# Decoder layer: the recurrence's chain in program order on TensorE, with the second half's preparation placed between its links

## The chip, the cores and the metric

The kernel runs on one core of a Trainium2 chip. The core has a matrix engine (TensorE, in the profile PE, with its weight loads as PEld), a vector engine (VectorE, DVE), a scalar engine (ScalarE, ACT), a general engine (GpSimd, POOL) and SyncE (SP), which here only issues DMAs. Each engine works through its own queue in the order in which the program was built, and semaphores hold an instruction back until what it needs is done. The metric is the device time of one execution in microseconds.

## What is computed

One decoder layer over 1024 tokens of width 1024, in float32. Half of the mixing width is attention in latent form (4 heads), the other half is a recurrence with a state of 64 by 64 for each of 8 heads. Cut to what matters here:

```python
u = rmsnorm(h, norm_pre_g)
p = u @ w_in
p_mla, p_rw, z = split(p)
# attention: latents, rotary parts, causal softmax -> y_mla
ps = p_rw + (token_shift(p_rw) - p_rw) * rw_mu
r, k, v, xw, xa = split(ps)
w_log = -softplus(-(rw_w0 + tanh(xw) @ rw_w2)) - 0.5
a = sigmoid(rw_a0 + xa @ rw_a2)

def step(S, inp):
    r_t, w_t, k_t, v_t, kk_t, a_t = inp
    sa = einsum('bhvk,bhk->bhv', S, -kk_t)
    S = (S * w_t[:, :, None, :] + sa[..., None] * (kk_t * a_t)[:, :, None, :]
         + v_t[..., None] * k_t[:, :, None, :])
    return S, einsum('bhvk,bhk->bhv', S, r_t)

_, ys = lax.scan(step, S0, xs)
y_rw = group_norm(ys) + bonus
out = concat([y_mla, y_rw]) * silu(z) @ w_out
h = h + rmsnorm(out, norm_post_g)
```

## The kernel before

The tokens are worked in two halves of 512. In each half the recurrence is cut into eight chunks of 64 tokens. Inside a chunk everything that doesn't depend on the state is done by matrix products ahead of time, which leaves a chain of eight short iterations that carry the state from chunk to chunk.

The program is a list of named steps, `PROGRAM` (line 129). A letter names a function, the digits are its arguments, the first of them the half:

- `A` (`stage_a`, line 154) loads four blocks of 128 tokens, sums their squares on ScalarE, takes the inverse root on GpSimd (`rstd`, lines 57 and 58, a power), scales on VectorE (line 170), transposes on TensorE (line 177, four transpositions to a tile, eight tiles in a half), and splits the result into a high part `uH` (ScalarE, line 181) and a low part `uL` (VectorE, line 182).
- `X` (`op_x`, `lora_in`, line 235) is the projection that feeds the two low-rank products; for half 0 it also loads their weights (`lora_load`, with splits on GpSimd, lines 232 and 233). A projection (`proj`, line 203) is 24 matmuls of 512 columns on line 210, with weights split on ScalarE (line 190) and GpSimd (line 200).
- `P` and `E` prepare one of four column blocks of a half: three projections and the low-rank products (lines 250 and 251, `lora_mm`), then the chunk products (`units`, lines 346 to 400).
- `I` inverts the chunk triangles (lines 401 to 456; VectorE at 418 to 421, TensorE at 447 and 454, copies at 455 and 456), with data sent through memory to other partitions.
- `C` is the chain (line 458). `N` and `G` are the group norm (line 501, reductions on VectorE, a power on GpSimd at line 510) and the outputs (line 518, transpositions on line 525).
- `Z` and `Y` are gate blocks (`zgate`, `zgate2`), `M` and `T` the attention's inputs and their transpositions (`mla_in`, `mla_tail`, with ScalarE's store copies on line 565), `B`, `U`, `K`, `J`, `Q` and `S` the rotary tables (lines 644 to 680), the attention and the output.

The written order is not the order that runs. The whole layer is built under a scheduler that simulates a timeline (line 41) and puts each engine's instructions in an order of its own; the place in the program is the priority. So work that is written later may be placed ahead of a waiting step, and two groups of one loop may be placed in turns.

One iteration of the chain, for two groups of heads (g of 0 and 1), each with a tile `pc` of its own in PSUM: TensorE multiplies the state, held in `SV`, with `LS` (line 474); ScalarE copies the result to `Rs` (line 476); TensorE does the other half of `LS` (line 480) into the same tile, then `AB` times `Rs` (line 484); ScalarE and VectorE copy that to `SV` (lines 486 and 487); TensorE does `BK` (line 490), VectorE adds it to the decayed state, which GpSimd made (lines 494 and 478), and TensorE ends with line 496, whose result ScalarE copies out (line 499). A link is one of these five groups; each is four matmuls in the program and eight records in the trace. What stands between the links is up to the scheduler.

Of the kernel before, what the change touches and what calls it, by code (L numbers as in the profile page):

```python
# [1 line left out]

# [14 lines left out]
T = 1024  # L17
# [27 lines left out]
def layer(tc, x, pos, w_in, w_out, w_uq, w_ukv, vecs, w2, a2, consts, post_g, out):  # L45
# [9 lines left out]
    def rstd(ss, scale):  # L55

        G.tensor_scalar(ss, ss, scale, EPS, ALU.mult, ALU.add)
        G.tensor_tensor(ss, ss, mhalf[:, 0:ss.shape[-1]], ALU.pow)
# [68 lines left out]
PROGRAM = (
    "A0 X0 Z00 B P00 E00 Z01 P01 E01 Z02 P02 E02 P03 E03 I0 C0 N00 G00 N01 G01 M0 Z03 Z04 Z05 Y06 T0 A1 X1",  # L130
    "P10 E10 Z10 P11 E11 Z11 P12 E12 P13 E13 I1 C1 N10 G10 N11 G11 M1 Z12 T1 Z13 Z14 Z15 Z16 Z17 U K J Q0",
    "Q1 Q2 Q3 S",
)

# [1 line left out]
def recurrence(tc, E):  # L136
# [11 lines left out]
    def col(c):  # L148
        return vec[:, c:c + 1]

    uH = alloc(P1, (128, 8, HALF), "uH", F32R)
    uL = alloc(P1, (128, 8, HALF), "uL", F32R)

    def stage_a(h):

        XT = (("v", "sq"), ("sg", "cs"), ("a", "k"), ("kf", "r"))
        for pr in range(2):
            xs = []
            for q in range(2):
# [5 lines left out]
                    junk = alloc(P1, (128, 512), "q", BF16)  # L165
                    S.activation(junk, xh[i], AF.Square, accum_out=ss[:, i:i + 1])
                G.tensor_tensor(ss[:, 0:1], ss[:, 0:1], ss[:, 1:2], ALU.add)
                E["rstd"](ss[:, 0:1], 1.0 / D)
                for i in range(2):
                    V.tensor_scalar(xh[i], xh[i], ss[:, 0:1], 1.0, ALU.mult, ALU.mult)  # L170
                xs.append(xh)
            for k2 in range(4):
                ps = pj((128, 2, 256))
                for kk in range(2):
                    kb = k2 * 2 + kk
                    for q in range(2):
                        PE.transpose(ps[:, kk, q * 128:(q + 1) * 128], xs[q][kb // 4][:, (kb % 4) * 128:(kb % 4 + 1) * 128], ident)
                for kk in range(2):
                    kb = k2 * 2 + kk
                    sl = slice(pr * 256, pr * 256 + 256)  # L180
                    S.activation(uH[:, kb, sl], ps[:, kk], AF.Copy, scale=col(V_PRE + kb))
                    V.scalar_tensor_tensor(uL[:, kb, sl], ps[:, kk], col(V_PRE + kb),  # L182
                                           uH[:, kb, sl].bitcast(F32), ALU.mult, ALU.subtract)

    def load_w(src, shape):
        wf = alloc(P1, shape, "wf", bufs=3)
# [13 lines left out]
                G.tensor_tensor(wl[:, sl], wf[:, sl], wh[:, sl].bitcast(F32), ALU.subtract)  # L200
        return wh, wl

    def proj(c0):

        wh, wl = load_w(w_in[:, c0:c0 + 128].rearrange("(k p) n -> p k n", p=128), (128, 8, 128))
        ps = pj()
# [1 line left out]
        for kb in range(8):  # L208
            for w_, u_ in ((wh, uH), (wh, uL), (wl, uH)):
                PE.matmul(ps, w_[:, kb], u_[:, kb], start=(n == 0), stop=(n == 23))  # L210
                n += 1
        return ps

    def shifted(ps, vi, tag, bufs):

# [17 lines left out]
            G.tensor_tensor(wl, wf, wh.bitcast(F32), ALU.subtract)  # L233

    def lora_in(h):
        px = shifted(proj(CO_X), V_MU_X, "v", 1)
# [5 lines left out]
        V.tensor_tensor(xw[64:128], th[0:64], xw[0:64].bitcast(F32), ALU.subtract)  # L242
        V.tensor_copy(xa[64:128], px[64:128])
        V.tensor_tensor(xa[0:64], px[64:128], xa[64:128].bitcast(F32), ALU.subtract)
        return xw, xa

    def lora_mm(nm, xx, cb):
        wh, wl = lora[nm]
# [206 lines left out]
                V.tensor_copy(AB[0:32, l, :, 32:64], pG[0:32])  # L455
                S.copy(AB[64:96, l, :, 32:64], pG[64:96])

    def chain(h, gt):

        for g in range(2):  # L460
            for e in range(2):
                G.tensor_copy(gt["g"][g]["SV"][ev[e], 0, e], Sst[ev[e], 2 * g:2 * g + 2])
        for c in range(NCH):

            pcs = [chp((128, 4, 2, 64)) for _ in range(2)]
            Rs = [alloc(P1, (128, 2, 64), "Rs", bufs=2) for _ in range(2)]
            SD = [alloc(P1, (128, 2, 64), "SD", bufs=2) for _ in range(2)]
            parts = []
            for g in range(2):
                LS, BK, AB, SV = (gt["g"][g][k] for k in ("LS", "BK", "AB", "SV"))  # L470
                parts.append((LS, BK, AB, SV, Sst[:, 2 * g:2 * g + 2], gt["Dg"][:, 2 * g:2 * g + 2], pcs[g], Rs[g], SD[g]))
            for LS, BK, AB, SV, St, Dg, pc, R_, D_ in parts:
                for l, e in le:
                    PE.matmul(pc[ev[e], 0, l], LS[:, l, c, e, 0:64], SV[:, c, e, l], start=(l == 0), stop=False,  # L474
                              skip_group_check=True)
                S.copy(R_, pc[:, 0])
                for e in range(2):
                    G.tensor_tensor(D_[ev[e]], SV[ev[e], c, e], bc(Dg[ev[e], :, c:c + 1], (64, 2, 64)), ALU.mult)  # L478
                for l, e in le:
                    PE.matmul(pc[ev[e], 1, l], LS[:, l, c, e, 64:128], SV[:, c, e, l], start=False, stop=False,  # L480
                              skip_group_check=True)
            for LS, BK, AB, SV, St, Dg, pc, R_, D_ in parts:
                for l, e in le:
                    PE.matmul(pc[ev[e], 2, l], AB[ev[e], l, c, 0:64], R_[ev[e], l], start=False, stop=False,
                              skip_group_check=True)
                S.copy(SV[ev[0], c, 0], pc[ev[0], 2])
                V.tensor_copy(SV[ev[1], c, 1], pc[ev[1], 2])  # L487
            for LS, BK, AB, SV, St, Dg, pc, R_, D_ in parts:
                for l, e in le:
                    PE.matmul(pc[ev[e], 3, l], BK[:, l, c, e], SV[:, c, e, l], start=False, stop=False,  # L490
                              skip_group_check=True)
                for e in range(2):
                    dst = SV[ev[e], c + 1, e] if c + 1 < NCH else St[ev[e]]
                    V.tensor_tensor(dst, pc[ev[e], 3], D_[ev[e]], ALU.add)  # L494
                for l, e in le:
                    PE.matmul(pc[ev[e], 1, l], AB[ev[e], l, c, 64:128], SV[ev[e], c, e, l], start=False,
                              stop=True, skip_group_check=True)

                S.copy(SV[:, c, 0], pc[:, 1])
# [561 lines left out]
```

## Time and profile before

| what | us |
|---|---|
| runs of the kernel | 783.88, 789.08, 786.29 |
| their median | 786.29 |
| the profiled execution's own time | 783.81 |
| its span | 782.0 |
| its mean granted TensorE clock (1 is full) | 0.951 |

A row of the profile's order of time gives the start in microseconds, the duration, the engine, the line, the operation, the tile written and the tiles read with their shapes, the count of merged instructions, and in square brackets the time for which the engine sat idle before it, with what ended that. Matmuls overlap in such rows, so the distance from one start to the next tells what a group costs, not its duration. A row of windows gives the stretch, its length, for each of TensorE, weight loads, VectorE, ScalarE and GpSimd the busy time (with the count), and behind them the granted clock, the DMA share and the rate. The stretch from the chain of half 0 to the end of its group norm runs here from about 232 to 354 us.

### The profile page before, as it was taken

What the parts mean: (1) busy time and instruction counts of PE and PEld (TensorE: products, weight loads), DVE (VectorE), ACT (ScalarE), POOL (GpSimd) and SP (SyncE); (2) the same over time, 40 slices, a digit from 0 to 9 for tenths busy, and PEclk for the clock granted to TensorE, in tenths of its full rate; (3) what the DMA queues carried; (4) which work ended last, traced back from release to release, by engine and by line L of the source; (5) the groups of instructions that cost most, each with busy time, mean ns of one, the idle gap of its engine ahead of it and who ended that gap; (6) DMA issues with size and microseconds to landing.
All of it is one profiled execution on the core that took longest, in us unless ns stands there. A gap on an engine that the chain in (4) does not pass through costs nothing. (4 is left out here: it accounts for less than half of the span.)

```text
span 782.0 us, 13855 instructions
## 1 busy us (share of the span) xinstructions
PE 713.0 (91%) x5136; PEld 586.1 (75%) x5136; DVE 466.4 (60%) x943; ACT 347.9 (44%) x877; POOL 331.9 (42%) x478
## 2 busy tenths in 40 slices
PE   2789999999978998889999989799899998899996
PEld 1667877789866776667888967577678997788885
DVE  4756757758925522495866691476497767644333
ACT  6465355343725453344353162426354566632221
POOL 6265645445942554263554374032332237442220
PEclk9999999999998899977999989879999999999999
DMA  6224241254383133043223366411023025144321
GB/s 208 80 69 115 54 114 51 68 151 134 114 187 89 28 108 83 2 89 85 57 68 97 86 171 156 131 44 42 2 55 101 21 89 162 52 166 141 121 82 54
DMA packets 118819, 72.84 MB, mean 93 GB/s; under 512 B 47072, under 2 KB 108256, under 8 KB 118752
## 3 DMA queue, kind: packets, MB, share of 16 engines
q1 hardware_dynamic: 118752, 71.96, 32.5%
q8 instruction: 40, 0.66, 0.4%
q14 instruction: 27, 0.22, 0.1%
HBM read 54.38 MB, written 17.56 MB: 92 GB/s over the span
## 5 line engine op out<-in xcount | busy, mean ns | idle before, releaser
L210 PE MATMUL pj<-uH,w 128*128 128x512 f32 x640 | 215.7, 411 | 3.3 <-DVE uL L182 2.5
L200 POOL TENSOR_TENSOR w<-wf,w 128x256 fp32r<-128x256 f32 x168 | 141.3, 871 | 116.6 <-ACT w L190 106.5
L210 PEld LDWEIGHTS pj<-uH,w 128*128 128x128 f32 x640 | 123.7, 195 | 33.1 <-DVE uL L182 2.9
L210 PE MATMUL pj<-uL,w 128*128 128x512 f32 x320 | 130.2, 407 | 0.0
L210 PEld LDWEIGHTS pj<-uL,w 128*128 128x128 f32 x320 | 62.6, 196 | 14.0 <-issue 0.8
L190 ACT CAST w<-wf 128x1024 fp32r<-128x1024 f32 (+1 forms) x50 | 51.4, 1027 | 28.8 <-PE pj L540 21.3
L478 POOL TENSOR_TENSOR SD<-SV,Dg 64x128 f32<-64x128 f32 x64 | 27.9, 436 | 74.0 <-DVE SV L494 59.9
L854 POOL TENSOR_SCALAR wf<-wf,sm 128x128 f32<-128x128 f32 (+7 forms) x32 | 24.0, 750 | 67.1 <-DVE sm L853 51.9
L198 POOL TENSOR_TENSOR w<-wf,w 128x224 fp32r<-128x224 f32 x32 | 23.8, 775 | 38.8 <-ACT w L190 32.2
L359 PEld LDWEIGHTS wk<-LS,pl 64*128 64x128 f32 x256 | 30.2, 191 | 12.5 <-issue 10.2
L979 DVE TENSOR_TENSOR LS<-pj,LS 128x512 f32<-128x512 f32 x16 | 11.1, 691 | 45.5 <-ACT cq L978 44.3
L359 PE MATMUL wk<-LS,pl 64*128 64x128 f32 x256 | 35.6, 289 | 1.3 <-DVE LS L317 1.2
L850 ACT ACTIVATE wf<-pj,mx 128x512 f32<-128x512 f32 (+3 forms) x48 | 27.7, 583 | 13.5 <-DVE mx L847 9.9
L865 ACT CAST BK<-wk 128x512 fp32r<-128x512 f32 (+3 forms) x48 | 22.4, 485 | 25.2 <-PE wk L863 23.2
L373 PEld LDWEIGHTS wk<-r,pl 64*128 64x128 f32 x256 | 29.5, 196 | 4.4 <-issue 2.9
L373 PE MATMUL wk<-r,pl 64*128 64x64 f32 x256 | 31.2, 284 | 1.2 <-DVE LS L364 1.0
L874 PE MATMUL ch<-BK,LS 128*128 128x256 f32 (+1 forms) x160 | 31.6, 282 | 0.7 <-ACT BK L865 0.7
L487 DVE COPY SV<-ch 64x128 f32<-64x128 f32 x32 | 9.2, 294 | 36.5 <-issue 25.7
L418 DVE TENSOR_TENSOR tmp<-XA 128x31 f32<-128x31 f32 (+15 forms) x62 | 28.2, 454 | 4.4 <-DMA XA<-sa 2.6
L866 DVE TENSOR_TENSOR AB<-wk,BK 128x512 fp32r<-128x512 f32 (+3 forms) x48 | 26.0, 551 | 7.3 <-ACT BK L865 6.8
L420 DVE TENSOR_TENSOR XA<-XA,tmp 128x31 f32<-128x31 f32 (+15 forms) x62 | 28.4, 458 | 1.9
L845 DVE TENSOR_REDUCE mx<-pj 128x1 f32<-128x512 f32 (+3 forms) x48 | 25.8, 551 | 6.0 <-PE pj L844 3.4
(339 smaller groups left out, 1659.4 us busy)
## 6 DMA issues: line engine op xcount, KB each, us to landing
wf<-in_w_in_dram SPq DMA_DIRECT2D x42, 512.0 KB, 3.9
zs<-st SPq DMA_DIRECT2D x16, 256.0 KB, 3.1
wf<-in_x_dram SPq DMA_DIRECT2D x8, 512.0 KB, 3.7
out_dram<-LS SPq DMA_DIRECT2D x16, 256.0 KB, 2.1
wf<-in_w_in_dram SPq DMA_DIRECT2D x8, 448.0 KB, 3.5
bvd<-st SPq DMA_DIRECT2D x8, 256.0 KB, 2.0
SV<-bvd SPq DMA_DIRECT2D x16, 128.0 KB, 3.4
yrw<-SV SPq DMA_DIRECT2D x8, 256.0 KB, 2.6
```

Of the source, the lines that this page charges most:

```text
L190: S.copy(wh, wf)
L200: G.tensor_tensor(wl[:, sl], wf[:, sl], wh[:, sl].bitcast(F32), ALU.subtract)
L210: PE.matmul(ps, w_[:, kb], u_[:, kb], start=(n == 0), stop=(n == 23))
L359: PE.matmul(pE[e][:, ci], pl[r, c4 + ci, 1 - e:3 - e].rearrange("p a b -> p (a b)"), LS[r, c4 + ci, e, :], start=True, stop=True)
L373: PE.matmul(pB[:, c], pl[r, c, 1 - e:3 - e].rearrange("p a b -> p (a b)"), dD[r, c], start=True, stop=True)
L418: V.tensor_tensor(t3, bc(At[:, j, j + 1:32].unsqueeze(2), (128, n, w)), bc(X[:, j, 0:w].unsqueeze(1), (128, n, w)), ALU.mult)
L420: V.tensor_tensor(X[:, j + 1:32, 0:w], X[:, j + 1:32, 0:w], t3, ALU.add)
L478: G.tensor_tensor(D_[ev[e]], SV[ev[e], c, e], bc(Dg[ev[e], :, c:c + 1], (64, 2, 64)), ALU.mult)
L845: V.tensor_reduce(mx[:, n5:n5 + 1], s_, axis=AX.X, op=ALU.min)
L850: S.activation(pr[:, b0:b1], sc[:, 0:b1 - b0], AF.Exp, bias=mx[:, 0:1], scale=-1.0, accum_out=sm[:, n5:n5 + 1])
L866: V.tensor_tensor(PL[:, b0:b0 + nb, o], pt[:, 0:nb], PH[:, b0:b0 + nb, o].bitcast(F32), ALU.subtract)
L874: PE.matmul(py[:, o], l_, r_, start=(j == 0 and n == 0), stop=(j == nk - 1 and n == 2), skip_group_check=True)
```

## The change

Four edits.

1. `stage_a` and `lora_in` become generators: they stop after each four transpositions, and after each two matmuls of a projection. `stage_a` leaves its last instruction on VectorE and on GpSimd in `last`.
2. The chain is wrapped so that TensorE's instructions in it keep the written order among themselves, and it takes an iterator `fill`. It draws one piece from it after line 484's links, one after the last link, and one more after each odd iteration. For half 0 the pieces are `A1` and then `X1`: eight pieces of transpositions and twelve of two matmuls, which is as many as there are places. For half 1 there are none.
3. In the main loop, whatever is written after `A0` is queued behind A0's last instructions on VectorE and on GpSimd, and whatever is written after `C0` is queued behind the chain's last matmul on TensorE.
4. `PROGRAM` is changed: `M0`, the gates and `T0` come before `C0`; `A1` and `X1` are gone as steps of their own; `P10` stands behind the group norms; `Y06` becomes `Z06 Z07`.

```diff
     def rstd(ss, scale):
         G.tensor_scalar(ss, ss, scale, EPS, ALU.mult, ALU.add)
-        G.tensor_tensor(ss, ss, mhalf[:, 0:ss.shape[-1]], ALU.pow)
+        return G.tensor_tensor(ss, ss, mhalf[:, 0:ss.shape[-1]], ALU.pow)
...
-        for op in " ".join(PROGRAM).split():
-            name = op.rstrip("0123456789")
-            ops[name](*(int(i) for i in op[len(name):]))
+        with contextlib.ExitStack() as order:
+            for op in " ".join(PROGRAM).split():
+                name = op.rstrip("0123456789")
+                last = ops[name](*(int(i) for i in op[len(name):]))
+                if op in ("A0", "C0"):
+
+                    for made in last:
+                        order.enter_context(tc.issue_after(made.ins))
...
-    "A0 X0 Z00 B P00 E00 Z01 P01 E01 Z02 P02 E02 P03 E03 I0 C0 N00 G00 N01 G01 M0 Z03 Z04 Z05 Y06 T0 A1 X1",
-    "P10 E10 Z10 P11 E11 Z11 P12 E12 P13 E13 I1 C1 N10 G10 N11 G11 M1 Z12 T1 Z13 Z14 Z15 Z16 Z17 U K J Q0",
+    "A0 X0 Z00 B P00 E00 Z01 P01 E01 Z02 P02 E02 P03 E03 I0 M0 Z03 Z04 Z05 Z06 Z07 T0 C0 N00 N01 P10 G00 G01",
+    "E10 Z10 P11 E11 Z11 P12 E12 P13 E13 I1 C1 N10 G10 N11 G11 M1 Z12 T1 Z13 Z14 Z15 Z16 Z17 U K J Q0",
...
-                E["rstd"](ss[:, 0:1], 1.0 / D)
+                last[1] = E["rstd"](ss[:, 0:1], 1.0 / D)
...
+                yield
                 for kk in range(2):
...
-                    V.scalar_tensor_tensor(uL[:, kb, sl], ps[:, kk], col(V_PRE + kb),
-                                           uH[:, kb, sl].bitcast(F32), ALU.mult, ALU.subtract)
+                    last[0] = V.scalar_tensor_tensor(uL[:, kb, sl], ps[:, kk], col(V_PRE + kb),
+                                                     uH[:, kb, sl].bitcast(F32), ALU.mult, ALU.subtract)
...
-    def proj(c0):
+    def proj_steps(c0, out):
...
+                if n % 2 == 0:
+                    yield
+        out.append(ps)
...
-    def chain(h, gt):
+    def chain(h, gt, fill):
...
-        for c in range(NCH):
+        with tc.manual_schedule(engines={PE.engine}):
+            for c in range(NCH):
...
+                next(fill, None)
...
+                next(fill, None)
+                if c % 2:
+                    next(fill, None)
+            for _ in fill:
+                pass
+        return [mm]
...
+    def op_a(h):
+        run(stage_a(h))
+        return last
+
     def op_x(h):
-        if h == 0:
-            lora_load()
-        xx[h] = lora_in(h)
+        lora_load()
+        run(lora_in(h))
+
+    def op_c(h):
+        return chain(h, gts[h], itertools.chain(stage_a(1), lora_in(1)) if h == 0 else iter(()))
```

The new lines shift the line numbers: 177 becomes 186, 210 becomes 220, 250 and 251 become 271 and 272, and the chain's 474, 480, 484, 490 and 496 become 497, 503, 507, 514 and 520.

What the scheduler makes of it is seen in the engines' orders. A row has the line, the operation, the tile written and the tiles read (a number tells buffers apart), the shape, and a count where equal instructions follow each other.

VectorE at the start of the program, before. The `q_330` rows are the rotary tables, `kf` and `r` the last block of input tokens, `uL` the low half of the transposed input:

```order
L655 CAST posf_327<-posi_325 128x8
L182 SCALAR_TENSOR_TENSOR uL_99<-pj_155,vec_65,uH_98 128x256
L661 TENSOR_SCALAR q_330<-cst_64,posf_327 128x32
L182 SCALAR_TENSOR_TENSOR uL_99<-pj_146,vec_65,uH_98 128x256
L661 TENSOR_SCALAR q_330<-cst_64,posf_327 128x32 x5
L170 TENSOR_SCALAR kf_178<-kf_178,ss_42_180 128x512
L170 TENSOR_SCALAR r_179<-r_179,ss_42_180 128x512
```

The same place now:

```order
L179 TENSOR_SCALAR k_165<-k_165,ss_37_166 128x512
L192 SCALAR_TENSOR_TENSOR uL_99<-pj_128,vec_65,uH_98 128x256
L192 SCALAR_TENSOR_TENSOR uL_99<-pj_137,vec_65,uH_98 128x256
L179 TENSOR_SCALAR kf_178<-kf_178,ss_42_180 128x512
L179 TENSOR_SCALAR r_179<-r_179,ss_42_180 128x512
L192 SCALAR_TENSOR_TENSOR uL_99<-pj_146,vec_65,uH_98 128x256
L192 SCALAR_TENSOR_TENSOR uL_99<-pj_128,vec_65,uH_98 128x256
```

The scaling of `kf` and `r` has moved up to the third transposed block; the table rows (line 701 now) begin only thirteen rows further down, behind the last `uL` of A0.

GpSimd there, before; `ss` is the sum of squares, `lora` the low-rank weights:

```order
L167 TENSOR_TENSOR ss_37_166<-ss_37_166 128x1
L57 TENSOR_SCALAR ss_37_166<-ss_37_166 128x1
L58 TENSOR_TENSOR ss_37_166<-ss_37_166,mhalf_74 128x1
L167 TENSOR_TENSOR ss_42_180<-ss_42_180 128x1
L232 TENSOR_SCALAR lora_228<-wf_229 128x512
L276 MEMSET sg_373 128x8
L57 TENSOR_SCALAR ss_42_180<-ss_42_180 128x1
L232 TENSOR_SCALAR lora_228<-wf_234 128x512
L233 TENSOR_TENSOR lora_228<-wf_229,lora_228 128x512
L58 TENSOR_TENSOR ss_42_180<-ss_42_180,mhalf_74 128x1
```

GpSimd there now:

```order
L176 TENSOR_TENSOR ss_37_166<-ss_37_166 128x1
L59 TENSOR_SCALAR ss_37_166<-ss_37_166 128x1
L60 TENSOR_TENSOR ss_37_166<-ss_37_166,mhalf_74 128x1
L176 TENSOR_TENSOR ss_42_180<-ss_42_180 128x1
L59 TENSOR_SCALAR ss_42_180<-ss_42_180 128x1
L60 TENSOR_TENSOR ss_42_180<-ss_42_180,mhalf_74 128x1
L250 TENSOR_SCALAR lora_228<-wf_229 128x512
```

The last block's power (the row with `mhalf`) now stands ahead of both low-rank splits; the other rows have gone behind it.

TensorE in an iteration of the chain of half 0 that had nothing else between its links, before. `ch` numbers tell the two groups apart:

```order
L474 MATMUL ch_2053<-SV_363,LS_360 64x64 x4
L474 MATMUL ch_2054<-SV_367,LS_364 64x64 x4
L480 MATMUL ch_2053<-SV_363,LS_360 64x64 x4
L484 MATMUL ch_2053<-Rs_2055,AB_362 64x64 x4
L480 MATMUL ch_2054<-SV_367,LS_364 64x64 x4
L484 MATMUL ch_2054<-Rs_2056,AB_366 64x64 x4
L490 MATMUL ch_2053<-SV_363,BK_361 64x64 x4
L490 MATMUL ch_2054<-SV_367,BK_365 64x64 x4
L496 MATMUL ch_2053<-SV_363,AB_362 64x64 x4
L496 MATMUL ch_2054<-SV_367,AB_366 64x64 x4
```

TensorE in the chain of half 0 now, from the third iteration's second group on; `pj` rows with line 186 are transpositions of half 1:

```order
L497 MATMUL ch_2301<-SV_367,LS_364 64x64 x4
L503 MATMUL ch_2301<-SV_367,LS_364 64x64 x4
L507 MATMUL ch_2300<-Rs_2302,AB_362 64x64 x4
L507 MATMUL ch_2301<-Rs_2303,AB_366 64x64 x4
L186 MATMUL pj_2344<-cst_64,a_2267 128x128
L186 MATMUL pj_2344<-cst_64,kf_2281 128x128
L186 MATMUL pj_2344<-cst_64,a_2267 128x128
L186 MATMUL pj_2344<-cst_64,kf_2281 128x128
L514 MATMUL ch_2300<-SV_363,BK_361 64x64 x4
L520 MATMUL ch_2300<-SV_363,AB_362 64x64 x4
L514 MATMUL ch_2301<-SV_367,BK_365 64x64 x4
L520 MATMUL ch_2301<-SV_367,AB_366 64x64 x4
```

The links of a group now follow each other, and the transpositions stand behind line 507's links and behind the last link.

TensorE further on, in the last iteration of that chain before; `wk` and `pj` rows are column blocks of half 1:

```order
L359 MATMUL wk_3049<-LS_2865,pl_2936 128x128 x4
L359 MATMUL wk_3050<-LS_2865,pl_2936 128x128 x4
L490 MATMUL ch_2115<-SV_363,BK_361 64x64 x4
L210 MATMUL pj_3297<-uH_98,w_3291 128x512
L210 MATMUL pj_3297<-uL_99,w_3291 128x512
L210 MATMUL pj_3297<-uH_98,w_3291 128x512
L490 MATMUL ch_2116<-SV_367,BK_365 64x64 x4
```

The chain's end now, with the last four matmuls of X1, the output transpositions (line 555) and the first low-rank product of half 1 (line 271):

```order
L514 MATMUL ch_2669<-SV_367,BK_365 64x64 x4
L520 MATMUL ch_2669<-SV_367,AB_366 64x64 x4
L220 MATMUL pj_2463<-uH_98,w_2457 128x512 x2
L220 MATMUL pj_2463<-uL_99,w_2457 128x512
L220 MATMUL pj_2463<-uH_98,w_2457 128x512
L555 MATMUL ch_2960<-cst_64,SV_363 128x64 x4
L555 MATMUL ch_2971<-cst_64,SV_363 128x64 x4
L555 MATMUL ch_2960<-cst_64,SV_363 128x64 x4
L555 MATMUL ch_2971<-cst_64,SV_363 128x64 x4
L271 MATMUL pj_2786<-xw_2743,lora_228 128x512
L272 MATMUL pj_2786<-xw_2743,lora_228 128x512
L271 MATMUL pj_2793<-xa_2744,lora_228 128x512
```

Half 1's blocks, which stood between the links before, now begin behind the chain.

More of the change, by code (lines that the diff above doesn't have):

```diff
@@ L1 @@
+import contextlib
+import itertools
 import math
@@ L152, in recurrence @@
     uL = alloc(P1, (128, 8, HALF), "uL", F32R)
+    last = [None, None]
     def stage_a(h):
@@ L211, in proj @@
                 n += 1
-        return ps
+                if n % 2 == 0:
+                    yield
+        out.append(ps)
+    def proj(c0):
+        out = []
+        for _ in proj_steps(c0, out):
+            pass
+        return out[0]
     def shifted(ps, vi, tag, bufs):
@@ L235, in lora_in @@
     def lora_in(h):
-        px = shifted(proj(CO_X), V_MU_X, "v", 1)
+        out = []
+        yield from proj_steps(CO_X, out)
+        px = shifted(out[0], V_MU_X, "v", 1)
         th = alloc(P1, (128, 512), "sq")
@@ L244, in lora_in @@
         V.tensor_tensor(xa[0:64], px[64:128], xa[64:128].bitcast(F32), ALU.subtract)
-        return xw, xa
+        xx[h] = xw, xa
     def lora_mm(nm, xx, cb):
@@ L462, in chain @@
                 G.tensor_copy(gt["g"][g]["SV"][ev[e], 0, e], Sst[ev[e], 2 * g:2 * g + 2])
-        for c in range(NCH):
[L465 to L499, printed above, removed]
@@ new lines, in chain @@
+        with tc.manual_schedule(engines={PE.engine}):
+            for c in range(NCH):
+                pcs = [chp((128, 4, 2, 64)) for _ in range(2)]
+                Rs = [alloc(P1, (128, 2, 64), "Rs", bufs=2) for _ in range(2)]
+                SD = [alloc(P1, (128, 2, 64), "SD", bufs=2) for _ in range(2)]
+                parts = []
+                for g in range(2):
+                    LS, BK, AB, SV = (gt["g"][g][k] for k in ("LS", "BK", "AB", "SV"))
+                    parts.append((LS, BK, AB, SV, Sst[:, 2 * g:2 * g + 2], gt["Dg"][:, 2 * g:2 * g + 2], pcs[g], Rs[g], SD[g]))
+                for LS, BK, AB, SV, St, Dg, pc, R_, D_ in parts:
+                    for l, e in le:
+                        PE.matmul(pc[ev[e], 0, l], LS[:, l, c, e, 0:64], SV[:, c, e, l], start=(l == 0), stop=False,
+                                  skip_group_check=True)
+                    S.copy(R_, pc[:, 0])
+                    for e in range(2):
+                        G.tensor_tensor(D_[ev[e]], SV[ev[e], c, e], bc(Dg[ev[e], :, c:c + 1], (64, 2, 64)), ALU.mult)
+                    for l, e in le:
+                        PE.matmul(pc[ev[e], 1, l], LS[:, l, c, e, 64:128], SV[:, c, e, l], start=False, stop=False,
+                                  skip_group_check=True)
+                for LS, BK, AB, SV, St, Dg, pc, R_, D_ in parts:
+                    for l, e in le:
+                        PE.matmul(pc[ev[e], 2, l], AB[ev[e], l, c, 0:64], R_[ev[e], l], start=False, stop=False,
+                                  skip_group_check=True)
+                    S.copy(SV[ev[0], c, 0], pc[ev[0], 2])
+                    V.tensor_copy(SV[ev[1], c, 1], pc[ev[1], 2])
+                next(fill, None)
+                for LS, BK, AB, SV, St, Dg, pc, R_, D_ in parts:
+                    for l, e in le:
+                        PE.matmul(pc[ev[e], 3, l], BK[:, l, c, e], SV[:, c, e, l], start=False, stop=False,
+                                  skip_group_check=True)
+                    for e in range(2):
+                        dst = SV[ev[e], c + 1, e] if c + 1 < NCH else St[ev[e]]
+                        V.tensor_tensor(dst, pc[ev[e], 3], D_[ev[e]], ALU.add)
+                    for l, e in le:
+                        mm = PE.matmul(pc[ev[e], 1, l], AB[ev[e], l, c, 64:128], SV[ev[e], c, e, l], start=False,
+                                       stop=True, skip_group_check=True)
+                    S.copy(SV[:, c, 0], pc[:, 1])
+                next(fill, None)
+                if c % 2:
+                    next(fill, None)
+            for _ in fill:
+                pass
@@ L593, in recurrence, with run @@
     lora, xx, gts, cqs, made = {}, {}, {}, {}, {}
+    def run(*steps):
+        for _ in itertools.chain(*steps):
+            pass
+    def op_a(h):
+        run(stage_a(h))
+        return last
     def op_x(h):
-        if h == 0:
-            lora_load()
-        xx[h] = lora_in(h)
+        lora_load()
+        run(lora_in(h))
+    def op_c(h):
+        return chain(h, gts[h], itertools.chain(stage_a(1), lora_in(1)) if h == 0 else iter(()))
     def op_p(h, cb):
@@ L611, in recurrence @@
     return {
-        "A": stage_a, "X": op_x, "P": op_p, "M": op_m, "T": lambda h: mla_tail(h, cqs[h]),
-        "E": op_e, "I": lambda h: inverse(h, gts[h]), "C": lambda h: chain(h, gts[h]),
+        "A": op_a, "X": op_x, "P": op_p, "M": op_m, "T": lambda h: mla_tail(h, cqs[h]),
+        "E": op_e, "I": lambda h: inverse(h, gts[h]), "C": op_c,
         "N": lambda h, g: group_norm(h, g, gts[h]), "G": lambda h, g: outputs(h, g, gts[h]), "Z": lambda h, b: zgate(h, b, b + 1),
```

## The prediction

> **What bounds the kernel now.** I read the page first, then TensorE's order of time through the start, the chain and the stretch behind it, with the other engines' rows there, and last the clock by windows.
>
> ```profile
> span 782.0 us, 13855 instructions
> PE 713.0 (91%) x5136; PEld 586.1 (75%) x5136; DVE 466.4 (60%) x943; ACT 347.9 (44%) x877; POOL 331.9 (42%) x478
> ```
>
> TensorE is busy for 91% and nobody else for more than 60%, so it is the bound, and its order is fixed when the kernel is built: a wait in front of one matmul delays all behind it. Time is to be won or lost only where TensorE waits or runs at half clock. The change touches three such places: the start, the chain of half 0, and the stretch behind that chain.
>
> The start, in TensorE's, VectorE's and GpSimd's order of time:
>
> ```profile
> 21.09 0.47 PE L177 MATMUL pj<-cst,kf 128*128 128x128 f32 x1 [3.42 <-DVE kf L170]
> 26.90 0.80 PE L210 MATMUL pj<-uH,w 128*128 128x512 f32 x1 [2.54 <-DVE uL L182]
> ...
> 17.00 3.64 DVE L661 TENSOR_SCALAR q<-cst,posf 128x32 f32<-128x32 f32 x5
> 20.56 0.48 DVE L170 TENSOR_SCALAR kf<-kf,ss 128x512 f32<-128x512 f32 x1
> ...
> 16.08 0.56 POOL L58 TENSOR_TENSOR ss<-ss,mhalf 128x1 f32<-128x1 f32 x1
> ```
>
> The last quarter of the input is scaled at 20.56, because the power on GpSimd that it needs ran at 16.08 and the table operations of line 661 filled VectorE until then. Transpositions and the first projection follow from it. Half a layer's markers are the four low-rank matmuls of line 250 that open each column block; the first and third of half 0 and of half 1 are:
>
> ```profile
> 43.63 0.77 PE L250 MATMUL pj<-xw,lora 128*128 128x512 f32 x1 [2.61 <-DVE xw L242]
> 109.26 0.39 PE L250 MATMUL pj<-xw,lora 128*128 128x512 f32 x1
> 256.70 0.79 PE L250 MATMUL pj<-xw,lora 128*128 128x512 f32 x1 [0.90 <-DVE xw L242]
> 366.88 0.39 PE L250 MATMUL pj<-xw,lora 128*128 128x512 f32 x1
> 367.12 0.40 PE L251 MATMUL pj<-xw,lora 128*128 128x512 f32 x1
> ```
>
> One iteration of the chain with nothing between its links, on TensorE, and its helpers on ScalarE and VectorE:
>
> ```profile
> 311.37 0.93 PE L474 MATMUL ch<-SV,LS 128*64 128x64 f32 x16
> 312.18 0.45 PE L480 MATMUL ch<-SV,LS 128*64 128x64 f32 x8
> 312.56 0.45 PE L484 MATMUL ch<-Rs,AB 64*64 64x64 f32 x8
> 312.94 0.45 PE L480 MATMUL ch<-SV,LS 128*64 128x64 f32 x8
> 313.32 0.45 PE L484 MATMUL ch<-Rs,AB 64*64 64x64 f32 x8
> 313.81 0.45 PE L490 MATMUL ch<-SV,BK 128*64 128x64 f32 x8
> 314.57 0.45 PE L490 MATMUL ch<-SV,BK 128*64 128x64 f32 x8 [0.31 <-DVE SV L487]
> 315.19 0.45 PE L496 MATMUL ch<-SV,AB 64*64 64x64 f32 x8 [0.17 <-DVE SV L494]
> 315.82 0.45 PE L496 MATMUL ch<-SV,AB 64*64 64x64 f32 x8 [0.17 <-DVE SV L494]
> 316.19 0.93 PE L474 MATMUL ch<-SV,LS 128*64 128x64 f32 x16
> ...
> 312.34 0.27 ACT L476 COPY Rs<-ch 128x128 f32<-128x128 f32 x1 [0.21 <-PE ch L474]
> ...
> 314.55 1.22 DVE L494 TENSOR_TENSOR SV<-ch,SD 64x128 f32<-64x128 f32 x4
> ```
>
> It takes 4.82 us (311.37 to 316.19). Ten groups go out at 0.38 each (312.18 to 312.56), 3.8 in sum, and 1.0 is waiting. It is that short because the links of group 0 and group 1 alternate: while the copy of line 476 or the addition of line 494 works for one, TensorE feeds the other.
>
> The clock, by windows (busy time of each engine, then the granted clock):
>
> ```profile
> 234.44:237.85 3.41, 2.52 (x52) 1.90 (x39) 1.92 (x5) 1.51 (x4) 1.11 (x2) 0.50 1.15 341
> 237.85:241.26 3.41, 3.18 (x20) 2.85 (x22) 1.64 (x4) 3.18 (x9) 0.00 (x0) 0.50 0.61 182
> 312.94:316.36 3.42, 2.73 (x57) 2.04 (x54) 1.75 (x6) 0.79 (x4) 0.93 (x3) 1.00 0.00 0
> 500.68:504.09 3.41, 2.69 (x29) 2.01 (x29) 3.29 (x7) 3.12 (x10) 0.00 (x0) 0.50 0.29 88
> 504.09:507.51 3.42, 2.58 (x28) 1.81 (x28) 1.73 (x5) 1.70 (x6) 0.32 (x1) 0.50 0.63 188
> ```
>
> The same chain at the same busy share (2.73 and 2.69 of 3.41) keeps the full clock once it has it, and stays at half where it began after a pause. Both chains begin at half.
>
> **The change, part by part.**
>
> *Start.* Later work may no longer pass A0's on VectorE and GpSimd: the line 661 operations (3.64 and more) and two steps of the loads' split go behind. The kf scaling can follow the k scaling as soon as its power is done, some 5 us earlier; lines 655 to 673 now sit where X0's matmuls cover them, for VectorE is needed again only after X0. Bounds 0 (if a wait of X0 for its split weights takes over) and 8; I take 5, nearest to the 3.64 and 2.54 that are quoted. It carries through to the inverse, since TensorE is full between.
>
> *Z06 Z07 for Y06.* 48 matmuls of 512 columns take the place of 96 of 256: the same columns in TensorE's stream, so I cost it at nothing; their loads keep their places on SP's queue ahead of the inverse's.
>
> *Where the chain begins.* Before, the first copy of line 476 stood behind ScalarE's store copies, and those behind DMAs:
>
> ```profile
> 231.49 0.48 ACT L565 COPY st<-pj 128x384 f32<-128x384 f32 x1 [2.10 <-DMA zs<-st]
> 237.54 1.03 ACT L565 COPY st<-pj 128x384 f32<-128x384 f32 x2 [1.69 <-DMA cTd<-st]
> 239.37 0.26 ACT L476 COPY Rs<-ch 128x128 f32<-128x128 f32 x1
> ```
>
> The copies stand ahead of it in the new order too, so the chain begins at 239.4 less 5, or 234.4. A1's eight loads, squares and scalings stay where they were on SP, ScalarE and VectorE, ahead of the chain; only its transpositions, their two halves and the projection move. What filled that pause (A1's transpositions) is gone from it: TensorE has almost nothing for some 7 us, so it begins at half clock, as before.
>
> *The chain's own pace.* In program order each group's links stand back to back. Line 480's work must wait for the copy of line 476: 0.21 after the matmuls, 0.27 of copying and 0.05, so 0.53, twice. Lines 484 to 490: 313.32 less 312.56 was filled by the other group; what is left open is 0.49, and that is where the first filling goes, free (four transpositions or two matmuls). Line 496's work waits for two additions (314.55, 1.22 for four, so 0.61) with 0.17 and 0.06 beside: 0.84, twice. Sum: 3.8 + 2×0.53 + 0.49 + 2×0.84 = 7.0 us, against 4.82. The second filling has nothing to hide behind: two matmuls of 512 columns take 0.48 (366.88 to 367.12 is one), and four transpositions, a quarter of the columns each but more instructions, are taken as the same (an estimate): twelve such fillings in eight iterations, less the little that their neighbours cover, 5.4 in all. ScalarE's and VectorE's halves of the transposed blocks stand between the links there, about 2 us over four iterations (an estimate: eight pairs of some 0.5, half of them in the way). So 8×7.0 + 5.4 + 2 − 0.8 = 62.6 us at full clock.
>
> At half clock a group takes 0.62 instead of 0.38:
>
> ```profile
> 511.19 0.70 PE L490 MATMUL ch<-SV,BK 128*64 128x64 f32 x8
> 511.82 0.69 PE L496 MATMUL ch<-SV,AB 64*64 64x64 f32 x8
> ```
>
> which adds about 2.4 to an iteration and doubles the fillings: 3.0 to 3.5 an iteration. The iterations with transpositions (the first three) are no denser than the windows at 500.68, so I let them stay at half: 9.5. From the fourth on, the fillings are full matmuls, and I let the clock come back. Bounds: 0 (full at once) and 25 (half to the end). Chain: 72 us; its end at 306.4.
>
> The Trainium skill, "TensorE: Matmul & The Clock Gate", part 4, says that transposes don't count as activity for the clock. The window at 237.85, mostly transpositions, was followed by full clock here, so the trace disagrees; by the page the 9.5 us would be certain.
>
> *Behind the chain.* Nothing later may pass it on TensorE, so P10 starts from nothing: line 250's matmuls wait for X1's last matmuls, ScalarE's work on them, and the group norm's share of ScalarE and VectorE. At the start this took 6.0 (37.61 to 43.63); now a group norm stands between:
>
> ```profile
> 37.61 0.69 ACT L217 ACTIVATE v<-pj,omm 128x512 f32<-128x512 f32 x1 [4.00 <-PE pj L210]
> ...
> 333.54 0.45 PE L496 MATMUL ch<-SV,AB 64*64 64x64 f32 x8
> 346.23 1.17 PE L525 MATMUL ch<-cst,SV 64*128 64x64 f32 x16
> ...
> 337.65 2.91 POOL L510 TENSOR_TENSOR gss<-gss,mhalf 128x16 f32<-128x16 f32 x1
> ```
>
> Before, the first output matmuls came 12.7 after the last link (333.54 to 346.23), the power on GpSimd (2.91) among what they waited for. Bounds 6 and 12.7; I take 9.5, the middle, as the norm's reductions and copies go ahead of line 250's operands on ScalarE and VectorE but its powers on GpSimd don't. Then the same blocks follow as in half 0, from first to third marker 65.6 (109.26 less 43.63), plus 1.5 for the output matmuls and for weight loads that SP now issues behind the outputs' store (hidden unless over 10 late, by the three loads already out). The third marker of half 1 comes at 306.4 + 9.5 + 67.1 = 383.0, against 366.88: 16.1 later. From there the same work is left in both, in nearly the same order, so the shift stays.
>
> *The chain of half 1* is written in the same order. Most of it is filled with attention; three iterations and a half have nothing between, as before:
>
> ```profile
> 555.80 0.93 PE L474 MATMUL ch<-SV,LS 128*64 128x64 f32 x16
> 560.63 0.93 PE L474 MATMUL ch<-SV,LS 128*64 128x64 f32 x16
> ```
>
> They go from 4.83 to 7.0: 7.6 more. Bounds 0 (waits covered by attention put there) and 16 (half clock as well).
>
> Sum: 783.8 + 16.1 + 7.6 = 807.5, with the start's 5 inside the 16.1. The profiled execution (783.81, span 782.0) lies 2.5 below the median of 786.29, which I don't correct for.
>
> **The rivals.**
>
> *Full clock* (the waits as above, no half clock in the chain). A dense filling right at the start could release the clock, as the window at 237.85 did, and the row at 312.94 shows that a chain then keeps it: 807.5 − 9.5 = 798. Against it stand the two windows from 500.68. [...]
>
> *Half clock to the end of the chain*, since even the fillings of the later iterations leave a third of each idle: 25 instead of 9.5 in chain 0, 8 more in chain 1: 823 to 831. For it: 500.68 to 507.51. Against: full matmuls follow every link from the fourth iteration on.
>
> *The chain is paced as before* (the other side). If the fillings fall exactly into the waits, an iteration costs 4.8 plus 0.7 of uncovered filling: 44 us, no clock loss, nothing in half 1. The marker comes at 234.4 + 44 + 76.6 = 355, 12 earlier: 772. It decides if line 480's and line 496's work needs no wait for the other engine's read of the same tile; the row at 315.19 has such a wait though the other group stood between, which speaks against it. Half of this gain, with full clock, gives about 785.
>
> **How the numbers follow.** Forecast (part half clock) 0.45, range 798 to 818; full clock 0.2; half clock throughout 0.12; paced as before 0.14; in between, about 785, 0.09. I predict 807. The range 784 to 826 leaves out the gain and the far end of the half clock, about 0.2. About 1% is what a measurement of this kernel can tell from no change: below 778 faster 0.16, within 0.1, above 794 slower 0.74.
>
> **What would show it.** Start: the kf scaling near 15 and the first marker near 38.5. Pace: iterations of 7 us without half clock, with waits of 0.5 before the second matmul group of each tile (named ScalarE's Rs) and 0.8 before its last (named VectorE's SV). Clock: half in the windows of the first three iterations. Behind: some 8 us nearly idle before line 271. The second half's chain: bare iterations of 7. The prediction is wrong if the bare iteration is under 6 us, or if the first marker of half 1 lies before 300.

## The result and the profile after

The changed kernel takes 826.2 us (median of four, 824.2 to 829.9) against 785.1 of the kernel before: a ratio of 1.0525, with a 95% interval from 1.046 to 1.059. It is 41 us slower. The forecast had the sign and the places, but not the size: 807 was predicted, and the time lies just above the upper end of the range (784 to 826), where one of the rivals (half clock to the end of the chain, 823 to 831) had put it. A trace is of one execution, and in the run below with transpositions in the pause that one is the slowest of its four (785.4 us, the others 773.3 to 779.0).

The head of the page after: span, busy time of each engine, and the granted clock in 40 slices of 20.6 us.

```profile
span 823.2 us, 13760 instructions
PE 731.1 (89%) x5088; PEld 598.9 (73%) x5088; DVE 468.9 (57%) x943; ACT 348.4 (42%) x876; POOL 337.9 (41%) x478
PEclk9999999999855655989999999798579999989999
```

TensorE has 48 instructions fewer and is busy for 18 us more, since matmuls at half clock count for longer. The clock row shows where: slices twelve to sixteen (226 to 329 us), which are the chain of half 0 and the stretch behind it, and a dip in slice 29 (576 to 597 us), which is the part of half 1's chain that has nothing between its links.

The order of time gives the points to lay beside those of the prediction. The start first, VectorE and then TensorE:

```profile
14.15 0.98 DVE L179 TENSOR_SCALAR kf<-kf,ss 128x512 f32<-128x512 f32 x1
...
36.30 0.77 PE L271 MATMUL pj<-xw,lora 128*128 128x512 f32 x1 [3.99 <-DVE xw L263]
319.96 0.80 PE L271 MATMUL pj<-xw,lora 128*128 128x512 f32 x1 [1.64 <-DVE xw L263]
387.71 0.39 PE L271 MATMUL pj<-xw,lora 128*128 128x512 f32 x1
```

The kf scaling is at 14.15 (20.56 before) and the first marker at 36.30 (43.63). One iteration of half 0's chain, the second, on TensorE:

```profile
240.37 0.63 PE L497 MATMUL ch<-SV,LS 128*64 128x64 f32 x8
241.35 0.69 PE L503 MATMUL ch<-SV,LS 128*64 128x64 f32 x8 [0.36 <-ACT Rs L499]
241.84 0.64 PE L497 MATMUL ch<-SV,LS 128*64 128x64 f32 x8
242.84 0.69 PE L503 MATMUL ch<-SV,LS 128*64 128x64 f32 x8 [0.36 <-ACT Rs L499]
243.47 1.12 PE L507 MATMUL ch<-Rs,AB 64*64 64x64 f32 x16
...
247.21 0.69 PE L520 MATMUL ch<-SV,AB 64*64 64x64 f32 x8 [0.95 <-DVE SV L518]
247.84 0.69 PE L514 MATMUL ch<-SV,BK 128*64 128x64 f32 x8
249.22 0.69 PE L520 MATMUL ch<-SV,AB 64*64 64x64 f32 x8 [0.69 <-DVE SV L518]
```

In half 0's chain every second link of a tile now stands behind a wait for ScalarE's copy, and every last link behind one for VectorE's addition. TensorE's waits over the whole program say the same (total in us, times, longest). Line 520 waits 18.3 us for VectorE and line 503 waits 13.5 us for ScalarE; their forerunners, lines 496 and 480, waited 3.0 and 0.6 us. After, then before:

```profile
PE ch L520 <- DVE SV L518: 18.3, 24, 1.7
PE ch L503 <- ACT Rs L499: 13.5, 25, 2.6
...
PE ch L496 <- DVE SV L494: 3.0, 16, 0.5
PE ch L480 <- ACT Rs L476: 0.6, 1, 0.6
```

And the links are slow as well: 0.49 to 0.63 apart where before it was 0.38. In the windows of the chain (length, busy time of TensorE, weight loads, VectorE, ScalarE and GpSimd, and the clock behind them) the clock is at half most of the time. It comes back twice, in the rows of 237.90 and 275.00, and is lost again:

```profile
237.90:241.30 3.40, 2.40 (x36) 1.77 (x36) 1.35 (x4) 1.27 (x4) 1.71 (x5) 0.88 0.00 0
245.00:260.00 15.00, 11.58 (x119) 8.93 (x118) 6.21 (x17) 5.41 (x15) 2.39 (x6) 0.50 0.01 1
260.00:275.00 15.00, 11.59 (x110) 8.50 (x108) 5.54 (x14) 5.26 (x14) 2.38 (x6) 0.51 0.00 1
275.00:290.00 15.00, 11.31 (x150) 8.15 (x150) 3.27 (x12) 2.60 (x10) 2.39 (x6) 0.71 0.00 1
292.50:313.00 20.50, 16.26 (x168) 11.52 (x168) 4.18 (x13) 3.62 (x13) 1.60 (x5) 0.50 0.00 1
```

In half 1 the iterations with nothing between their links have gone from 4.83 to 8.68 us:

```profile
581.14 0.69 PE L497 MATMUL ch<-SV,LS 128*64 128x64 f32 x8
589.82 0.69 PE L497 MATMUL ch<-SV,LS 128*64 128x64 f32 x8
```

They didn't begin at half clock. The first of them still has links of 0.45 us, and the clock falls inside it, at about 575. The links first, then the windows around them, then the same stretch of the kernel before, which stays at full clock:

```profile
573.96 0.45 PE L503 MATMUL ch<-SV,LS 128*64 128x64 f32 x8 [0.80 <-ACT Rs L499]
574.24 0.40 PE L497 MATMUL ch<-SV,LS 128*64 128x64 f32 x8
575.01 0.69 PE L503 MATMUL ch<-SV,LS 128*64 128x64 f32 x8 [0.37 <-ACT Rs L499]
...
550.00:572.70 22.70, 17.90 (x228) 14.87 (x224) 12.73 (x37) 11.96 (x49) 4.76 (x11) 0.92 0.13 36
572.70:603.00 30.30, 21.00 (x288) 16.73 (x286) 8.52 (x27) 8.25 (x30) 5.22 (x14) 0.54 0.00 1
...
545.00:567.00 22.00, 18.87 (x355) 14.38 (x354) 8.51 (x27) 9.08 (x37) 6.94 (x17) 1.00 0.01 2
```

So the 41.2 us between the two spans build up in three steps: −7.3 up to the first marker, +28.1 from there to the third marker of half 1 (which is 20.8 late, 387.71 against 366.88), and +20.4 from there to the end, in which half 1's chain lies.

### The profile page after: what moved, and what is told of

The parts are those of the page before. It is cut to its first block, busy times and chain, and to the rows that moved or that the text cites. A ratio compares the mean times of both kernels' runs of the same rounds, so it can differ in the third digit from the quotient of the medians.

```text
span 823.2 us, 13760 instructions
## 1 busy us (share of the span) xinstructions
PE 731.1 (89%) x5088; PEld 598.9 (73%) x5088; DVE 468.9 (57%) x943; ACT 348.4 (42%) x876; POOL 337.9 (41%) x478
## 5 line engine op out<-in xcount | busy, mean ns | idle before, releaser
L220 PE MATMUL pj<-uH,w 128*128 128x512 f32 x672 | 230.4, 417 | 1.3 <-ACT plast L238 1.3
L210 POOL TENSOR_TENSOR w<-wf,w 128x256 fp32r<-128x256 f32 x168 | 143.2, 883 | 108.5 <-ACT w L200 100.8
L220 PEld LDWEIGHTS pj<-uH,w 128*128 128x128 f32 x672 | 131.6, 198 | 31.9 <-ACT plast L238 1.7
L220 PE MATMUL pj<-uL,w 128*128 128x512 f32 x336 | 138.2, 411 | 0.0
L220 PEld LDWEIGHTS pj<-uL,w 128*128 128x128 f32 x336 | 66.7, 199 | 14.7 <-issue 0.5
L208 POOL TENSOR_TENSOR w<-wf,w 128x224 fp32r<-128x224 f32 x32 | 23.6, 769 | 38.1 <-ACT w L200 31.6
L520 PE MATMUL ch<-SV,AB 64*64 64x64 f32 x256 | 19.2, 289 | 19.7 <-DVE SV L518 18.3
L380 PEld LDWEIGHTS wk<-LS,pl 64*128 64x128 f32 x256 | 28.0, 187 | 11.7 <-issue 10.2
L380 PE MATMUL wk<-LS,pl 64*128 64x128 f32 x256 | 33.1, 284 | 0.8 <-DVE LS L385 0.8
L520 PEld LDWEIGHTS ch<-SV,AB 64*64 64x64 f32 x256 | 13.8, 182 | 25.8 <-DVE SV L518 22.6
L503 PE MATMUL ch<-SV,LS 128*64 128x64 f32 x256 | 20.2, 303 | 13.6 <-ACT Rs L499 13.5
L439 DVE TENSOR_TENSOR tmp<-XA 128x31 f32<-128x31 f32 (+15 forms) x62 | 28.1, 454 | 4.0 <-DMA XA<-sa 2.0
```

Source lines behind the costliest of these rows:

```text
L380: PE.matmul(pE[e][:, ci], pl[r, c4 + ci, 1 - e:3 - e].rearrange("p a b -> p (a b)"), LS[r, c4 + ci, e, :], start=True, stop=True)
L439: V.tensor_tensor(t3, bc(At[:, j, j + 1:32].unsqueeze(2), (128, n, w)), bc(X[:, j, 0:w].unsqueeze(1), (128, n, w)), ALU.mult)
L520: mm = PE.matmul(pc[ev[e], 1, l], AB[ev[e], l, c, 64:128], SV[ev[e], c, e, l], start=False, stop=True, skip_group_check=True)
```

## The experiments

In all of them the kernel before ran on the same chip; its median was 787.4 in the first batch of four and 783.5 in the second of three, so ratios are given. Differences are those between the medians; by the ratios they come out up to some 2 us larger or smaller.

**Links in turns.** In the changed kernel only the loops of the chain are cut differently, so that the two groups take turns as they did before. Fillings, barriers and the program's list stay.

```diff
                     S.copy(R_, pc[:, 0])
...
+                for LS, BK, AB, SV, St, Dg, pc, R_, D_ in parts:
                     for l, e in le:
                         PE.matmul(pc[ev[e], 1, l], LS[:, l, c, e, 64:128], ...)
-                for LS, BK, AB, SV, St, Dg, pc, R_, D_ in parts:
                     for l, e in le:
                         PE.matmul(pc[ev[e], 2, l], AB[ev[e], l, c, 0:64], ...)
...
                         V.tensor_tensor(dst, pc[ev[e], 3], D_[ev[e]], ALU.add)
+                for LS, BK, AB, SV, St, Dg, pc, R_, D_ in parts:
                     for l, e in le:
                         mm = PE.matmul(pc[ev[e], 1, l], AB[ev[e], l, c, 64:128], ...)
```

> The changed kernel with the links of the two groups written in turns again in both halves' chains (first links of both groups, then the second and third of each, then the fourth of both, then the last of both), the fillings at the same places. Theory (back-to-back links expose the waits, and the thin chain then keeps half clock): the chain of half 0 falls from 83 us to 47 to 52, bare iterations of half 1 from 8.7 to 4.8, in all 770 to 782 us. Rival (half 1's column blocks, which now begin only behind the chain, are what costs): the chain gets shorter but the time stays above 812. Rival (the cold start alone keeps the clock at half whatever the order): chain about 72, in all about 805.

Measured: 774.1 us, a ratio of 0.985 (0.981 to 0.989) to the kernel before: 52 us from the changed kernel to this one, and 1.5% faster than the kernel before. Half 0's chain took 49.8 us (236.67 to 286.42, the first of the second links to the last link) where the changed kernel needs 80.1 (232.02 to 312.16). (From the very first link, as the 83 of the expectation is counted, they are 54.3 and 83.5; the expected 47 to 52 is met by the one count and missed by the other.) TensorE in this run, some links of half 0's chain and a bare iteration of half 1 (line 503 is 504 here, 520 is 521):

```profile
236.67 0.64 PE L504 MATMUL ch<-SV,LS 128*64 128x64 f32 x8
...
241.69 0.45 PE L521 MATMUL ch<-SV,AB 64*64 64x64 f32 x8 [0.96 <-DVE SV L518]
242.31 0.45 PE L521 MATMUL ch<-SV,AB 64*64 64x64 f32 x8 [0.17 <-DVE SV L518]
...
286.42 0.45 PE L521 MATMUL ch<-SV,AB 64*64 64x64 f32 x8 [0.17 <-DVE Sst L518]
...
543.82 0.93 PE L497 MATMUL ch<-SV,LS 128*64 128x64 f32 x16
548.65 0.93 PE L497 MATMUL ch<-SV,LS 128*64 128x64 f32 x16
```

Half 1's iteration is back at 4.83. In half 0 the clock came back within the first iteration, though the start was as cold, and unlike in the changed kernel it stayed (the windows as above):

```profile
234.50:237.90 3.40, 1.71 (x26) 1.48 (x26) 0.00 (x0) 1.37 (x4) 0.00 (x0) 0.50 0.86 254
241.30:244.70 3.40, 2.71 (x51) 2.13 (x52) 1.87 (x6) 1.82 (x6) 1.70 (x5) 1.00 0.00 0
244.70:248.10 3.40, 2.31 (x46) 1.73 (x42) 2.07 (x7) 1.79 (x6) 0.00 (x0) 1.00 0.02 5
```

So neither the late start of half 1's blocks, which stand behind the chain here too, nor the cold start by itself is what costs. The order of the links is.

**Dead matmuls in the waits.** To tell the waits from the clock, the changed kernel's order is kept and matmuls of 512 columns, whose results nobody reads, are put where half 0's chain waits. They are 48, six in each of eight iterations, and the trace has 48; the 96 of the expectation is a miscount.

```diff
+        def dead(n):
+            if h == 0:
+                for _ in range(n):
+                    PE.matmul(wk(), lora["w"][0][:, 0:128], lora["w"][0], start=True, stop=True)
...
+                    dead(1)
                     for l, e in le:
                         PE.matmul(pc[ev[e], 1, l], LS[:, l, c, e, 64:128], SV[:, c, e, l], ...)
...
+                    dead(2)
                     for l, e in le:
                         mm = PE.matmul(pc[ev[e], 1, l], AB[ev[e], l, c, 64:128], ...)
```

> The changed kernel with dead matmuls of 512 columns put into the waits of half 0's chain: one before each second link, two before each last link (96 in all, results unread). Theory (the clock stays at half because the chain is thin): the windows of the chain go to full clock, the chain takes 62 to 68 us instead of 83, in all 806 to 814 us. Rival (the clock doesn't depend on how thin the chain is, or the chain's length is set by ScalarE and VectorE alone): the chain takes 83 to 90 us, in all 825 to 833.

Measured: 806.7 us, a ratio of 1.025 (1.022 to 1.028): with more work in it the kernel is 19.5 us faster than without. The chain took 60.3 us (235.79 to 296.12; 64.5 from the very first link), and its windows are at full clock from 245 on (line 503 is 507 here, 520 is 525, and the dead matmuls are 483):

```profile
235.79 0.70 PE L507 MATMUL ch<-SV,LS 128*64 128x64 f32 x8 [2.78 <-ACT Rs L502]
296.12 0.45 PE L525 MATMUL ch<-SV,AB 64*64 64x64 f32 x8
...
245.00:260.00 15.00, 13.93 (x184) 9.48 (x183) 8.05 (x22) 6.89 (x22) 3.06 (x8) 1.00 0.01 2
260.00:275.00 15.00, 14.89 (x186) 9.55 (x184) 6.57 (x18) 6.02 (x18) 3.32 (x9) 1.00 0.00 1
```

That splits half 0's chain: 80.1 less 60.3, about 20 us, is the clock; 60.3 less 49.8, about 10, is the waits at full clock. The dead matmuls stand in waits that are there anyway; what they add all the same makes the 10 an upper end and the 20 a lower one.

**Half 1's chain left to the scheduler.** In the changed kernel the written order holds for half 0 only.

```diff
-        with tc.manual_schedule(engines={PE.engine}):
+        with tc.manual_schedule(engines={PE.engine}) if h == 0 else contextlib.nullcontext():
```

> The changed kernel with the written order kept only in half 0's chain; half 1's chain is left to the scheduler as in the kernel before. Theory (half 1's chain costs 18 to 21 us by its order and clock): 803 to 810 us. Rival (half 1's end is late only because it starts late, the order is covered by attention): 820 to 830.

Measured: 807.6 us, a ratio of 1.027 (1.024 to 1.030), 18.6 less than the changed kernel. Its third marker of half 1 is at 387.29, as late as in the changed kernel, so all of that is won behind it.

**Links in turns, half 1 free.** The edit of the first run of this section and the one just above together.

> Links in turns as in the run before last, but half 1's chain left to the scheduler. Theory (in turns the written order is as good as the scheduler's in half 1): 770 to 778 us, within 0.5% of 774. Rival (the scheduler's placing of attention between the links of half 1 is better, or worse): a difference of 5 us or more either way.

Measured: 775.7 us, a ratio of 0.989 (0.982 to 0.997), not to be told from the 774.1. With the changed kernel and the three runs of these two edits the two halves are apart: with half 1 free, half 0 back to back costs 807.6 less 775.7, or 32 us; with half 0 back to back, half 1 back to back costs 18.6.

**The start alone.** The kernel before, with one of the two barriers: what is written after A0 is queued behind its last instructions on VectorE and GpSimd.

```diff
+        with contextlib.ExitStack() as order:
...
+                last = ops[name](*(int(i) for i in op[len(name):]))
+                if op == "A0":
+                    for made in last:
+                        order.enter_context(tc.issue_after(made.ins))
```

> The kernel before with one part of the change: work written after the first half's stage A is queued behind that stage's last instructions on VectorE and GpSimd. Theory (the start's 7.3 us carry through to the end): 776 to 781 us, about 0.9% faster than before, first marker near 36.5. Rival (a later wait takes them back): within 0.3% of before.

Measured: 781.0 us, a ratio of 0.993 (0.990 to 0.996). The first marker is at 36.39, 7.2 earlier, and 5.7 of that (0.7% of 787.4; 3.5 to 7.9 by the interval) arrive at the end. The expected range ended where the time lies, at 781.

**Transpositions in the pause before the chain.** On top of the links in turns, the eight pieces of transpositions are drawn ahead of the chain.

```diff
+        for _ in range(8):
+            next(fill, None)
         with tc.manual_schedule(engines={PE.engine}):
```

> Links in turns, and the eight pieces of transpositions drawn ahead of half 0's chain, so that they may stand in the pause before it; the chain keeps the twelve pieces of matmuls. Theory (the pause before the chain, some 10 us, hides them, and each piece between links costs its own 0.4): 3 to 5 us less than the links in turns alone, 769 to 772. Rival (their halves on ScalarE and VectorE hold up the copies that the chain's start waits for): no gain or slower, 774 to 780.

Measured: 777.6 us, a ratio of 0.990 (0.983 to 0.996): no gain over the links in turns (0.985) is to be seen, so the theory fell. The time lies in the rival's range; the rival's reason was not followed up. In the profiled execution TensorE is nearly full from 231 on, about half of it with transpositions, the rest with the end of the inverse (line 475) and the first links, and the clock stays at half. It stays there after the last transposition too (243.98), among links and matmuls of 512 columns, even where TensorE is busy all the time (row of 251.50):

```profile
231.00:234.50 3.50, 3.16 (x71) 2.58 (x66) 1.70 (x4) 1.66 (x5) 1.15 (x3) 0.50 1.12 344
234.50:237.90 3.40, 3.26 (x26) 2.62 (x26) 0.48 (x1) 1.43 (x5) 0.00 (x0) 0.50 0.58 171
251.50:255.00 3.50, 3.50 (x36) 2.52 (x34) 0.59 (x2) 0.78 (x3) 0.00 (x0) 0.50 0.00 0
245.00:260.00 15.00, 13.75 (x126) 9.44 (x128) 4.41 (x14) 3.04 (x11) 3.18 (x8) 0.50 0.01 1
```

**The gate pair.** The changed kernel with `Y06` in place of `Z06 Z07`.

```diff
-... Z03 Z04 Z05 Z06 Z07 T0 C0 ...
+... Z03 Z04 Z05 Y06 T0 C0 ...
```

> The changed kernel with the pair of gate blocks of half 0 computed together again (96 matmuls of 256 columns in place of 48 of 512). Theory (the same columns in the same stream): 824 to 829 us, within 0.3% of the changed kernel. Rival (the pair's smaller share of pauses before the chain changes the chain's start): 3 us or more off.

Measured: 825.8 us, a ratio of 1.051 (1.044 to 1.058). This part of the change costs nothing that can be measured.

The barrier behind `C0` and the other moves in the program's list were not run by themselves. They all stand in the run with the links in turns, which is faster than the kernel before, so they don't bring the loss.

## Why the prediction fell short

- **The start** was put at 5 and came to 7.3 at the first marker. Mechanism right, size a little low. The run with this part alone shows that 5.7 of it reach the end.
- **The gate pair** was put at nothing, and no cost of it can be measured.
- **The chain's beginning**: the copy that was expected at 234.4 comes at 231.7 (239.37 before), earlier by the start's gain and a little more, with TensorE idle before it and the clock at half, as predicted.

```profile
231.70 0.27 ACT L499 COPY Rs<-ch 128x128 f32<-128x128 f32 x1
```

- **The pace at full clock** was right: 62.6 us were worked out, and the run with dead matmuls, at full clock but for its first iteration, took 60.3. The one iteration of the changed kernel's chain that ran almost wholly at full clock, the fifth, took 7.5 us from its first link to the next iteration's, which is the 7.0 and the 0.48 of a filling. (The waits were put at 0.53 and 0.84 and are 0.36 and 0.69, and the 0.8 that the sum takes off is not explained there.)

```profile
273.97 0.70 PE L497 MATMUL ch<-SV,LS 128*64 128x64 f32 x8
281.45 0.69 PE L497 MATMUL ch<-SV,LS 128*64 128x64 f32 x8
```

- **The step that failed** is the clock: the chain "keeps the full clock once it has it", and so "From the fourth on, the fillings are full matmuls, and I let the clock come back." That was read from the kernel before, where the links take turns. Back to back the clock came back only for short stretches and was lost again (0.88 in the row of 237.90, 0.71 in that of 275.00), and the run with dead matmuls shows that the half clock of half 0's chain is worth 20 us, not the 9.5 of the sum; by the sum itself it is 17.9 (80.5 from the first copy to the last link, less 62.6). Two matmuls between links didn't hold the clock: in the row of 292.50, where all fillings are matmuls, TensorE is busy for 16.26 of 20.50 us and at half. The prediction had rows for this (500.68 to 507.51, half at 75 to 79%), named the case and gave it 0.12.
- **Behind the chain** 9.5 were taken; from the last link to line 271 it took 7.8 (312.16 to 319.96), and the blocks behind it 67.75 where 67.1 were worked out. Both were about right.
- **Half 1's chain** is the larger miss, and only in part by the same step. The sum gave 807.5 and the profiled execution took 824.95; of these 17.5 us, 4.7 are there at the third marker (383.0 and 387.71) and 12.8 come behind it, where 7.6 were put in and 20.4 were measured, outside the bounds of 0 and 16. The chain's first link, the fifth iteration's first link and the second link of the second group in the eighth, of before and then of after:

```profile
500.07 0.45 PE L474 MATMUL ch<-SV,LS 128*64 128x64 f32 x8 [2.12 <-ACT AB L456]
550.89 0.45 PE L474 MATMUL ch<-SV,LS 128*64 128x64 f32 x8
567.03 0.45 PE L480 MATMUL ch<-SV,LS 128*64 128x64 f32 x8
...
518.73 0.45 PE L497 MATMUL ch<-SV,LS 128*64 128x64 f32 x8 [0.62 <-ACT AB L477]
572.71 0.45 PE L497 MATMUL ch<-SV,LS 128*64 128x64 f32 x8
601.71 0.70 PE L503 MATMUL ch<-SV,LS 128*64 128x64 f32 x8 [1.04 <-ACT Rs L499]
```

The bare stretch went from 16.1 (550.89 to 567.03) to 29.0 us, so 12.9 of the 20.4 are bare iterations. The prediction priced them at full clock, 7.0; they began at full clock, lost it in the first of them, and then took 8.68. That is 5.3 of the 12.8 (12.9 less 7.6). The mixed iterations ahead of it grew by 3.2 (50.8 to 54.0): "Most of it is filled with attention" held roughly. The way from the third marker to the chain's first link shrank by 2.2, and the way from 601.71 to the end grew by 6.5, which is not traced to a cause. The run with half 1 free brings back 18.6 in all.

With half clock in both chains the sum of the prediction would have read 783.8 + 31.6 + 16, or 831 (its own 25 for 9.5, its own 16 for 7.6). That this comes close to 826 is in part luck, as the 25 is 5 to 7 too large and the 16 is 4 too small. For half 0 the choice between two bounds failed; for half 1 neither bound held. The rival on the other side, that the fillings would fall into the waits, falls: the waits of 0.36 and 0.69 are there in every iteration of half 0's chain, with the fillings elsewhere.

## What to carry to other kernels

A written order on the engine that is the bound has to keep the turns that a scheduler had made: two independent groups whose links alternate hide each other's round trips to other engines, and the same links in the order in which the loops read don't. Count the round trips of the written order from the old trace before freezing it. And where such waits thin out TensorE's stream for some tens of microseconds, price it at half clock, also where it begins at full: in the changed kernel the links back to back lost the full clock each time they had it (at about 240, 281 and 575 us), and the same links in turns kept it.

## What the runs showed of the hardware

- More matmuls made the kernel faster: 48 dead ones in the waits of half 0's chain took 19.5 us off, and the clock in the chain went from 0.50 and 0.51 to 1.00 (rows of 245.00 and 260.00 in both).
- The clock can fall without a long idle. Half 1's bare iterations, back to back, lost it at about 575 us, with waits of no more than 0.80 us in the six microseconds before. The Trainium skill, "TensorE: Matmul & The Clock Gate", part 1, gives half clock after an idle window of some 3.4 us. The same part of that page of the Trainium skill also tells of a kernel whose frequent short idles between groups of matmuls made the clock swing, and this is nearer to what is seen here.
- How thin a stretch may be is not told by the busy time of a window alone: in turns the clock stayed full at 2.31 busy of 3.40 us (244.70), back to back it was lost in a window with 2.40 of 3.40 (237.90), and in the one traced execution with transpositions ahead it stayed at half at 3.50 of 3.50 (251.50). What decides it stays open.
- Whether transpositions can bring the clock back isn't settled either. The Trainium skill, "TensorE: Matmul & The Clock Gate", part 4, says that the full clock doesn't set in for them. In the run with transpositions ahead it didn't, but it didn't in windows without any either, and the window at 237.85 of the kernel before, mostly transpositions and quoted in the prediction, was followed by full clock.
